# One forward pass on Trainium2: first loads reordered, 128-row matmuls in the mLSTM heads, another PEER chunk order, matmuls without a reader in two norms

## The chip, the cores and the metric

The kernel runs on one core of one Trainium2 chip, as one program. The metric is the device time of that program in microseconds. The core has five engines that work from queues of their own: TensorE (PE in the rows, with its weight loads as PEld), VectorE (DVE), ScalarE (ACT), GpSimd (POOL) and SyncE (SP, which here issues almost all loads). TensorE multiplies into PSUM; a weight load puts a stationary operand of up to 128 rows by 128 columns into the array, and a matmul streams a moving operand of up to 512 columns through it.

## What is computed

The reference runs 256 tokens of width 1024 in float32 through two blocks. The first block has two layers: a mixer (an mLSTM in layer 0, latent attention in layer 1), a layer norm over the residual, a PEER feed-forward with its own norm, and a gated per-layer embedding. The second block is a hybrid attention and a SwiGLU feed-forward. Cut to the parts that the change touches:

```python
def mlstm_mixer(x, w_in, b_if, hn_g, w_out):          # 8 heads, q and k of 64, v of 128
    proj = x @ w_in                                   # q, k, v, input and forget gate, output gate
    b = cumsum(log_sigmoid(forget gate))              # the kernel: all 256 tokens in one go
    log_w[t, s] = b[t] - b[s] + ig[s], s <= t         # M[t] = running max of ig - b
    qk = (q @ k.T) * exp(log_w - m)                   # per head, causal
    h = (qk @ v) / max(|sum(qk)|, exp(-m))
    return (sigmoid(og) * head_norm(h)) @ w_out

x = layer_norm(ALPHA * x + mix, ln_g, ln_b)           # "norm 0" after layer 0's mixer, "norm 2" after layer 1's

def peer_ffn(x, w_q, sub_keys, u, v):                 # once per layer, 16384 experts
    ...                                               # top 16 of a product of two sets of 128 keys, 8 heads
    act = gelu(x @ u[expert])
    out = sum(gate * act * v[expert])
```

The kernel computes PEER densely: the gate weights are put into a 16384 x 256 matrix that is zero where an expert wasn't picked, and all experts are run through it.

## The kernel before

Nearly all matrix products are float32 products of three passes: `split` (line 127) rounds a tile to `hi` on ScalarE and forms the rest `lo` on VectorE (or GpSimd), both of type fp32r, and `mm3` (line 153) adds hi·hi, hi·lo and lo·hi with lines 159, 160 and 161. A few small products are plain float32 matmuls, which the hardware runs as two passes each. Weights come in slabs of 1 MB: `prep` (line 131) loads a slab on SP's queue into one of three `raw` buffers and splits it in two halves, into 8 `hi` and 7 `lo` buffers. `linT` (a slab stationary, 256 tokens moving) and `linN`/`accN` (tokens stationary, 512 columns of a slab moving) consume them.

The code is straight-line Python. A framework places each instruction on its engine's queue, in an order that follows the program's order and its own estimate of readiness, and puts in the waits; buffers of a tag rotate, and a pool that is opened after another was closed may take over its memory, and then waits for its last reader. `issue_after` holds an instruction back in that ordering until another one is placed.

**The start.** `setup` (line 96) loads the small constants `vecs`. `load_x` (line 405) loads x transposed in four parts of 256 KB and splits it in eight. `trig_tables` (line 804) loads the positions and computes a table that only layer 1 needs. `mlstm` (line 414) loads the gate weights (512 KB), the q and k weights (four slabs), x again by rows (`B.X`, 1 MB) and the head norm's gain `hn` (512 KB). On TensorE it runs the gate product (24 matmuls), q and k (192), v, and then the heads. From the gate product VectorE and ScalarE make the rows `ig`, `Bc` and their running maximum `M` (lines 449 to 469).

**The heads.** `head_a` (line 493) makes for one head the exponent `lw` (line 499: `sel`, 8 rows, picks the head's row of M; line 500 adds the causal mask) and the product `qk` (line 501, 64 rows: two heads share the 128 partitions of `kT`), for two blocks of 256 and 128 columns. `head_b` multiplies by v. Between them lie three steps of the output gate's product.

**The norms.** `post_norm` (line 239) takes the two token halves (`tb`) one after the other: statistics on VectorE, normalised rows, eight transposes on TensorE (line 265), then per 128 columns the split of the transposed rows on ScalarE, VectorE and GpSimd (lines 271 to 276). With `rows` (norms 0 and 2) it also updates `B.X` on VectorE (lines 286 and 287). What follows both norms is PEER's query product `peer_w_q`, whose first slab is split before the norm and the second one after those X updates.

**PEER.** 64 chunks of 256 experts. `u_pair` makes gelu(x @ u) of a chunk (96 matmuls of 256 columns); the down product takes 24 of 512 columns. The first 25 chunks' `u_pair` (NPRE) run early, among the selection and the building of the gate matrix, and lie in `pre`. The gate matrix goes to DRAM (`wd`, 16 writes of 1 MB) and comes back in groups of four chunks (`wt`, line 783, two buffers). The last loop then takes the chunks in order: `up(j)` returns `pre[j]` or runs `u_pair`, one chunk ahead of the down product of the chunk before. In layer 0 that loop also carries 24 steps of the second block's `Ada` product, a load of 1 MB each, at every other chunk from 8 on.

Of the kernel before, what the change touches and what calls it, by code (L numbers as in the profile page):

```python
# [22 lines left out]
P = 128  # L23
# [28 lines left out]
class Builder:  # L52
# [43 lines left out]
    def setup(self):  # L96
        nc, c = self.nc, self.const
        self.ident = self.t(c, [P, P], F32, "ident")
        make_identity(nc, self.ident)
        self.vecs = self.t(c, [P, self.A["vecs"].shape[1]], F32, "vecs")  # L100
        nc.sync.dma_start(self.vecs, self.A["vecs"])
# [28 lines left out]

    def prep(self, name, s, lo_engine=None):

# [4 lines left out]
        raw = self.t(self.raw_p, [P, k, n], F32, "raw")  # L137
        self.nc.sync.dma_start(raw, src)
        if name in BY_K or k * n <= 1024 or n <= P:
# [75 lines left out]
    def rsqrt(self, var, eps, shape, tag="rs", scale=1.0):  # L215
# [13 lines left out]
        return r  # L229

    @contextmanager
    def behind(self):
# [6 lines left out]
    def post_norm(self, acc, i, rows):  # L239
# [6 lines left out]
        for tb in range(2):  # L246
# [10 lines left out]
            for h in range(2):  # L257
# [6 lines left out]
                for k in range(4 * h, 4 * h + 4):  # L264
                    nc.tensor.transpose(ps[tb, h][:, (k % 4) * P:(k % 4 + 1) * P], Y[:, tb, k * P:(k + 1) * P],
                                        self.ident)
        for tb in range(2):
# [137 lines left out]
def load_x(B):  # L405
    nc = B.nc
    B.x32 = B.t(B.state, [P, KD, S], F32, "x32")
    for k in range(0, KD, 2):
        nc.sync.dma_start(B.x32[:, k:k + 2, :], B.A["xT"][:, k:k + 2, :])
        for i in range(k, k + 2):  # L410
            B.split(B.x32[:, i, :], B.xT[0][:, i, :], B.xT[1][:, i, :])


def mlstm(B):
# [3 lines left out]
    act = B.act  # L418
    with B.pool("ml") as p, B.pool("mlw", 2) as w:
# [8 lines left out]
        sel = B.t(p, [8, 8, P], F32, "sel")  # L428
        nc.gpsimd.memset(sel, 0.0)
        nc.gpsimd.affine_select(out=sel, in_=sel, pattern=[[1, 8], [0, P]], compare_op=OP.not_equal, fill=-1.0,  # L430
                                base=0, channel_multiplier=-1)
        v.memset(va[:, :, :, 128:129], 1.0)
        hn = B.t(p, [P, D], F32, "hn")
        nc.sync.dma_start(hn, A["hn_g"].to_broadcast([P, D]))
        nc.gpsimd.tensor_scalar(hn, hn, 0.5, None, op0=OP.mult)

# [10 lines left out]
        ab = B.t(p, [32, S], F32, "ab")  # L447
        e = B.t(p, [32, S], F32, "e")
        u = B.t(p, [32, S], F32, "u")
# [8 lines left out]
        v.scalar_tensor_tensor(lf, z, 0.0, lf, op0=OP.min, op1=OP.subtract)  # L458
        zero = B.t(p, [32, S], F32, "zero")
        v.memset(zero, 0.0)  # L460
        ab2 = B.t(p, [64, S], F32, "ab2")
# [3 lines left out]
        v.tensor_tensor(ab2[0:32, :], ig, Bc, op=OP.subtract)  # L465
        M = B.t(p, [32, S], F32, "M")
# [12 lines left out]
        for tb in range(2):  # L479
# [4 lines left out]
        act(flo, tok[:, :, 32:40], AF.Exp, scale=-1.0)  # L484
        acc = B.linN(B.xT, "a_w_v")
        for tb in range(2):
# [6 lines left out]
        def head_a(h):  # L493
            r0, c = 64 * (h % 2), h // 2
# [90 lines left out]
def peer(B, li):  # L585
# [4 lines left out]
    with ExitStack() as es:  # L590
# [175 lines left out]
        with B.pool("wp", 2) as wp, B.pool("dn", 2) as dn, ExitStack() as es4:  # L766
# [7 lines left out]
            extra = Ada(B, es4.enter_context(B.pool("ada"))) if li == 0 else None  # L774
            nxt = up(0)
            last = []
            for j in range(NPAIR):
                g = nxt
                if j + 1 < NPAIR:
                    nxt = up(j + 1)  # L780
                if j % 4 == 0:
# [11 lines left out]
                last.append(((ah, al), B.slab("peer_v", li * NPAIR + j), 0, 2))  # L793
                if j != NPAIR - 2:
                    B.accN(acc, last, j == 0, j == NPAIR - 1)
                    last = []
                if extra and 8 <= j < 56 and j % 2:
                    extra.step(j // 2 - 4)
                    if j == 55:
                        extra.finish()  # L800
# [3 lines left out]
def trig_tables(B):  # L804
# [3 lines left out]
    with B.pool("tr") as p:  # L808
        pi = B.t(p, [P, S], I32, "pi")
        nc.sync.dma_start(pi, B.A["positions"].to_broadcast([P, S]))  # L810
        ang = B.t(p, [P, S], F32, "ang")
        n = B.t(p, [P, S], F32, "n")
        v.tensor_copy(ang, pi)
        v.tensor_scalar(ang, ang, B.vec("inv_freq"), None, op0=OP.mult)
        magic = 12582912.0
# [704 lines left out]
def build(tc, A, out, stages=ALL):  # L1520
    with ExitStack() as ctx:
# [3 lines left out]
        load_x(B)  # L1525
        trig_tables(B)
        if "a0" in stages:
            mlstm(B)
        else:
            B.nc.sync.dma_start(B.X, A["x"])  # L1530
        if "b0" in stages:
            peer(B, 0)
# [45 lines left out]
```

## Time and profile before

| | us |
|---|---|
| median of three runs (lowest, highest) | 2439.83 (2435.09, 2444.13) |
| the profiled execution | 2436.32 |
| its span, first to last instruction | 2434.3 |
| TensorE busy | 2354.2 (97% of the span) |
| VectorE, ScalarE, GpSimd busy | 1655.3, 1231.7, 134.2 |

In a timeline row stand the start in the span, the duration (of all that the row merges), engine, line, operation, output and inputs with their shapes, and the count; in brackets the idle time of that engine before it, and what ended that. Matmuls overlap: one of 256 columns has a duration of 0.28 us, but the next starts 0.12 us after it, so what a matmul costs is the distance between starts. A row of a table of stretches has the stretch, its length, the busy time and the count of instructions started for PE, PEld, DVE, ACT and POOL, then the granted TensorE clock as a share of 2.4 GHz, the busy share of the DMA engines and GB/s. A row of waits has who waited for whom, the sum in us, how often, and the longest.

### The profile page before, as it was taken

How to read it: one execution, taken by the hardware profiler on the slowest of the kernel's cores; microseconds unless marked ns; L12 is line 12 of the kernel's file. 1: busy time of each engine (PE TensorE's matmuls, PEld its weight loads, DVE VectorE, ACT ScalarE, POOL GpSimd, SP SyncE). 2: the span in 40 equal slices, each digit the busy share in tenths (PEclk: the TensorE clock that was granted, in tenths of full speed). 3: DMA queues.
4: the chain of work that ended last, by engine and by line, in shares of the span. 5: the costliest groups of instructions: out<-in, count | busy, mean ns of one | idle time of the engine just before them, and what ended most of it. 6: DMA issues, size and time to landing. Idle time of an engine off the chain costs nothing.

```text
span 2434.3 us, 40711 instructions
## 1 busy us (share of the span) xinstructions
PE 2354.2 (97%) x16430; PEld 2152.7 (88%) x16430; DVE 1655.3 (68%) x3164; ACT 1231.7 (51%) x1813; POOL 134.2 (6%) x117
## 2 busy tenths in 40 slices
PE   7989998999999999999999999999999999999998
PEld 6789998889999998988989888999999888789998
DVE  5679995876666665767999576555555584658554
ACT  5554555444444444745555444444444474556442
POOL 1054000000000000006300000000000010000000
PEclk9999999999999999999999999999999999999999
DMA  7333677886677664434367766655655444125543
GB/s 280 111 135 137 242 289 254 318 313 260 253 264 269 248 235 166 158 138 144 134 243 281 256 237 233 213 214 197 225 208 197 166 170 169 70 88 181 184 155 104
DMA packets 134205, 495.23 MB, mean 203 GB/s; under 512 B 8064, under 2 KB 76032, under 8 KB 80896
## 3 DMA queue, kind: packets, MB, share of 16 engines
q1 hardware_dynamic: 129120, 458.55, 52.4%
q10 hardware_dynamic: 4896, 34.08, 3.4%
q8 instruction: 128, 2.10, 0.3%
q14 instruction: 61, 0.50, 0.1%
HBM read 457.99 MB, written 34.60 MB: 202 GB/s over the span
## 4 chain that ended last, share of the span: by engine, by line
PE 47%; DVE 1%; ACT 1%; DMA 1%; issue 0%; DVEq 0%; SPq 0%; ACTq 0%
PE ps L160 9%; PE ps L161 9%; PE ps L159 9%; PE acc L159 5%; PE acc L160 5%; PE acc L161 5%; PE ps L1258 1%; PE acc L1271 0%; DMA wt<-wd 0%; PE ps L756 0%; PE acc L1144 0%; DVE lo L129 0%; PE ps L757 0%; PE ps L1259 0%; PE ps L1004 0%
## 5 line engine op out<-in xcount | busy, mean ns | idle before, releaser
L78 ACT ACTIVATE hi<-raw 128x1024 fp32r<-128x1024 f32 (+1 forms) x754 | 772.0, 1044 | 816.3 <-PE ps L160 353.7
L129 DVE TENSOR_TENSOR lo<-raw,hi 128x1024 fp32r<-128x1024 f32 (+1 forms) x714 | 865.4, 1219 | 456.6 <-PE ps L161 269.5
L159 PE MATMUL ps<-s,hi 128*128 128x256 f32 x3248 | 921.5, 285 | 15.9 <-ACT hi L78 13.3
L161 PE MATMUL ps<-s,lo 128*128 128x256 f32 x3248 | 919.4, 283 | 8.3 <-DVE lo L129 8.3
L160 PE MATMUL ps<-s,hi 128*128 128x256 f32 x3248 | 921.7, 284 | 2.0 <-DVE s L276 1.5
L159 PEld LDWEIGHTS ps<-s,hi 128*128 128x128 f32 x3248 | 615.4, 190 | 22.1 <-ACT hi L78 13.7
L161 PEld LDWEIGHTS ps<-s,lo 128*128 128x128 f32 x3248 | 615.6, 190 | 10.5 <-DVE lo L129 10.4
L160 PEld LDWEIGHTS ps<-s,hi 128*128 128x128 f32 x3248 | 616.3, 190 | 7.0 <-issue 2.0
L159 PE MATMUL acc<-hi,ah 128*128 128x512 f32 x1024 | 401.1, 392 | 10.3 <-ACT ah L78 10.2
L160 PE MATMUL acc<-lo,ah 128*128 128x512 f32 x1024 | 401.4, 392 | 0.0
L161 PE MATMUL acc<-hi,al 128*128 128x512 f32 x1024 | 400.8, 392 | 0.0
L159 PEld LDWEIGHTS acc<-hi,ah 128*128 128x128 f32 x1024 | 193.4, 189 | 49.6 <-ACT ah L78 11.5
L161 PEld LDWEIGHTS acc<-hi,al 128*128 128x128 f32 x1024 | 193.4, 189 | 41.3 <-DVE al L129 0.6
L160 PEld LDWEIGHTS acc<-lo,ah 128*128 128x128 f32 x1024 | 193.2, 189 | 37.7
L78 ACT ACTIVATE ah<-aw 128x512 fp32r<-128x512 f32 x128 | 80.3, 627 | 99.4 <-DVE aw L789 62.0
L129 DVE TENSOR_TENSOR al<-aw,ah 128x512 fp32r<-128x512 f32 x128 | 88.3, 690 | 55.4 <-ACT ah L78 54.6
L276 POOL TENSOR_TENSOR s<-x,s 128x128 fp32r<-128x128 f32 x48 | 24.3, 520 | 1545.9 <-ACT x L78 1533.2
L129 POOL TENSOR_TENSOR lo<-raw,hi 128x1024 fp32r<-128x1024 f32 x40 | 98.3, 2476 | 23.4 <-PE ps L161 12.8
L789 DVE TENSOR_TENSOR aw<-g,wt 128x256 f32<-128x256 f32 x156 | 59.3, 422 | 32.3 <-ACT g L78 32.3
L756 PE MATMUL ps<-oh,o 128*128 128x128 f16 x512 | 65.7, 220 | 9.6 <-DVE oh L750 5.3
L78 ACT ACTIVATE st<-ps 128x512 f32<-128x512 f32 x128 | 66.7, 605 | 1.8 <-ACT pre L78 1.7
L78 ACT ACTIVATE g<-ps 128x512 f32<-128x512 f32 (+1 forms) x82 | 46.5, 567 | 39.1 <-PE ps L161 39.1
(461 smaller groups left out, 2383.7 us busy)
## 6 DMA issues: line engine op xcount, KB each, us to landing
raw<-in_peer_u SPq DMA_DIRECT2D x128, 1024.0 KB, 4.8
raw<-in_peer_v SPq DMA_DIRECT2D x128, 1024.0 KB, 4.9
wd<-st ACTq DMA_DIRECT2D x32, 1024.0 KB, 4.7
wt<-wd SPq DMA_DIRECT2D x32, 1024.0 KB, 6.0
raw<-in_w_ada SPq DMA_DIRECT2D x24, 1024.0 KB, 5.2
raw<-in_peer_w_q SPq DMA_DIRECT2D x16, 1024.0 KB, 4.9
raw<-in_ffn_gate SPq DMA_DIRECT2D x11, 1024.0 KB, 4.8
raw<-in_ffn_up SPq DMA_DIRECT2D x11, 1024.0 KB, 4.8
```

Source lines behind the costliest of these rows:

```text
L78: i = self.nc.scalar.activation(out, in_, func, **kw)
L129: (lo_engine or self.nc.vector).tensor_tensor(lo, src, hi.bitcast(F32), op=OP.subtract)
L159: mm(out, lhsT[0], rhs[0], start=first, stop=False)
L160: mm(out, lhsT[0], rhs[1], start=False, stop=False)
L161: mm(out, lhsT[1], rhs[0], start=False, stop=last)
L276: lo = (v if tb and k % 2 == 0 else nc.gpsimd).tensor_tensor(xT[1][:, k, ts], x32[:, k, ts], xT[0][:, k, ts].bitcast(F32), op=OP.subtract)
L756: mm(ps[:, i * P:(i + 1) * P], o2[:, t // 2, :, t % 2], oh1[:, t // 2, :, t % 2], start=True, stop=False)
L789: v.tensor_tensor(aw[:, sl].rearrange("p (g t) -> p g t", t=16), g[:, sl].rearrange("p (g t) -> p g t", t=16), wt[:, :, (j % 4) * 2 + i, : ...
L1258: mm(o, qa[r0:r0 + 64, c, tb * P:(tb + 1) * P], kk[r0:r0 + 64, :n], start=True, stop=False)
```

## The change

- The load of `vecs` moves from `setup` into `load_x`, behind the second part of x. The gate weights are loaded first of all, on ScalarE's queue, and split before x.
- `B.X`, `hn` and `trig_tables` move behind the v product; the halving of `hn` goes from GpSimd to VectorE.
- `kT` gets one slot of 128 rows per head, of which 64 stay zero (a memset on GpSimd); q's two heads of a pair stay in `qT` as before. `sel` becomes 128 rows of fp32r, and M is split into two fp32r rows `Mp` of 128 partitions, so that line 499 runs twice, as hi and lo, and every matmul of `head_a` contracts over 128 rows.
- Tokens' transposes (`tok`) come behind the v product. Some tiles share memory (`e`, `M`, `zero`, `n`), and the pool of the heads' work tiles is closed before the one of the norm's rows is opened.
- `post_norm` 0 and 2: behind the transposes of the first token half 11 matmuls of 512 bf16 columns, behind those of the second half 4, into a PSUM buffer that nothing reads.
- Both PEER loops take the chunks in the order 28 to 31, 0 to 27, 32 to 63. `Ada`'s steps stay at the same places in the sequence.

```diff
+    def prep(self, name, s, lo_engine=None, queue=None):
...
+        (queue or self.nc.sync).dma_start(raw, src)
...
+    def stoke(self, n, after):
+        with self.tc.issue_after(after):
+            o = self.psum("acc")
+            for _ in range(n):
+                self.nc.tensor.matmul(o, self.ident_b, self.ident_b.unsqueeze(1).to_broadcast([P, 4, P]),
+                                      start=True, stop=True)
...
+                    tr = nc.tensor.transpose(ps[tb, h][:, (k % 4) * P:(k % 4 + 1) * P], Y[:, tb, k * P:(k + 1) * P],
+                                             self.ident)
+            if i % 2 == 0:
+                self.stoke(4 if tb else 11, tr.ins)
...
 def load_x(B):
+    B.prep("a_w_gate", 0, None, nc.scalar)
     for k in range(0, KD, 2):
         nc.sync.dma_start(B.x32[:, k:k + 2, :], B.A["xT"][:, k:k + 2, :])
+        if k == 2:
+            nc.sync.dma_start(B.vecs, B.A["vecs"])
...
-        for n, i in (("a_w_gate", 0), ("a_w_qk", 0)):
-            B.prep(n, i)
-        nc.sync.dma_start(B.X, A["x"])
+        B.prep("a_w_qk", 0)
-        kT = B.t(p, [P, 4, S], F32, "kT")
+        kT = B.t(p, [P, 8, S], F32, "kT")
+        nc.gpsimd.memset(kT, 0.0)
...
+        sel = B.t(p, [P, 8, P], F32R, "sel")
+        Mp = B.t(p, [P, 2, S], F32R, "Mp")
+        s32 = B.t(B.hi_p, [P, 8, P], F32, "hi")
...
+        act(sel, s32, AF.Copy)
...
+        B.split(M, Mp[0:32, 0, :], Mp[0:32, 1, :])
...
-                act(kT[:, c - 4, :], ps, AF.Copy, scale=0.125)
+                for r0 in (0, 64):
+                    act(kT[r0:r0 + 64, 2 * (c - 4) + r0 // 64, :], ps[r0:r0 + 64, :], AF.Copy, scale=0.125)
 
         B.linT(B.xT, "a_w_qk", range(4), ev_qk)
+        acc = B.linN(B.xT, "a_w_v")
+        trig_tables(B)
+        nc.sync.dma_start(B.X, A["x"])
+        hn = B.t(p, [P, D], F32, "hn")
+        nc.sync.dma_start(hn, A["hn_g"].to_broadcast([P, D]))
+        v.tensor_scalar(hn, hn, 0.5, None, op0=OP.mult)
...
-                mm(lw[:, o], sel[:, h, :], M[0:8, sb * P:], start=True, stop=False)
+                for i in range(2):
+                    mm(lw[:, o], sel[:, h, :], Mp[:, i, sb * P:], start=i == 0, stop=False)
                 mm(lw[:, sb * S:sb * S + P], B.ident_b, B.smask_b, start=False, stop=True)
-                mm(qk[:, o], kT[r0:r0 + 64, c, sb * P:(sb + 1) * P], qT[r0:r0 + 64, c, sb * P:], start=True, stop=True)
+                mm(qk[:, o], kT[:, h, sb * P:(sb + 1) * P], qT[:, c, sb * P:], start=True, stop=True)
...
+        es.close()
         with B.pool("rows") as rows:
...
+            order = [*range(28, 32), *range(28), *range(32, NPAIR)]
+            nxt = up(order[0])
             last = []
-            for j in range(NPAIR):
+            for n, j in enumerate(order):
                 g = nxt
-                if j + 1 < NPAIR:
-                    nxt = up(j + 1)
+                if n + 1 < NPAIR:
+                    nxt = up(order[n + 1])
```

## Rows read from the trace of the kernel before

**Rows 1.** What TensorE waited for, first 45 us.
```profile
PE ps L159 <- ACT hi L78: 12.0, 2, 10.1
PE ps L161 <- DVE lo L129: 3.5, 4, 1.7
```

**Rows 2.** Timeline of TensorE, start to the end of q and k.
```profile
10.11 0.58 PE L159 MATMUL ps<-s,hi 128*128 128x256 f32 x1 [10.11 <-ACT hi L78]
...
17.31 0.39 PE L161 MATMUL ps<-s,lo 128*128 128x256 f32 x1 [1.71 <-DVE lo L129]
...
43.87 0.34 PE L481 MATMUL ps<-ident,ab 64*128 64x64 f32 x2
```

**Rows 3.** Table of stretches: q and k without a wait.
```profile
31.00:43.00 12.00, 12.00 (x104) 12.00 (x104) 11.66 (x16) 9.35 (x14) 0.00 (x0) 1.00 0.75 269
```

**Rows 4.** Timelines of ScalarE and VectorE at the start.
```profile
4.57 2.26 ACT L78 ACTIVATE s<-x 128x256 fp32r<-128x256 f32 x6 [2.48 <-DMA x<-in_xT]
...
9.00 1.06 ACT L78 ACTIVATE hi<-raw 128x1024 fp32r<-128x1024 f32 x1 [0.75 <-DMA raw<-in_a_w_gate]
...
11.49 2.00 ACT L78 ACTIVATE hi<-raw 128x1024 fp32r<-128x1024 f32 x2 [1.43 <-DMA raw<-in_a_w_qk]
...
15.44 0.29 DVE L813 CAST ang<-pi 128x256 f32<-128x256 int32 x1 [4.12 <-DMA pi<-in_positions]
```

**Rows 5.** DMA rate in 40 slices of 0.3 us, first 12 us.
```profile
GB/s 0 0 0 0 0 0 155 201 171 171 212 191 205 328 376 389 348 301 280 225 239 273 212 355 451 328 492 437 451 437 437 410 382 311 297 184 89 181 44 174
```

**Rows 6.** Timeline of TensorE, one head's products (head_b, then head_a).
```profile
74.95 0.61 PE L511 MATMUL ps<-va,ex 128*128 128x129 f32 x4
75.40 0.39 PE L513 MATMUL ps<-va,ex 128*128 128x129 f32 x2
75.71 0.69 PE L499 MATMUL ps<-M,sel 8*128 8x256 f32 x2
...
76.50 0.92 PE L501 MATMUL ps<-qT,kT 64*128 64x256 f32 x4
77.35 0.48 PE L499 MATMUL ps<-M,sel 8*128 8x128 f32 x2
...
77.80 0.48 PE L159 MATMUL acc<-hi,s 128*128 128x512 f32 x1
```

**Rows 7.** Timelines of TensorE and VectorE around norm 0.
```profile
143.55 1.90 PE L265 MATMUL ps<-ident,s 128*128 128x128 f32 x8 [2.93 <-DVE s L260]
...
156.18 0.39 PE L161 MATMUL ps<-s,lo 128*128 128x256 f32 x1 [1.61 <-DVE lo L129]
...
150.10 2.62 DVE L286 TENSOR_TENSOR s<-s,gr 128x1024 f32<-128x1024 f32 x2
```

**Rows 8.** Around norm 2: timelines of TensorE and GpSimd, and a stretch.
```profile
1111.75 1.09 PE L265 MATMUL ps<-ident,s 128*128 128x128 f32 x8 [2.62 <-DVE s L260]
...
1123.70 0.39 PE L161 MATMUL ps<-s,lo 128*128 128x256 f32 x1 [0.78 <-DVE lo L129]
...
1117.79 1.37 POOL L276 TENSOR_TENSOR s<-x,s 128x128 fp32r<-128x128 f32 x1
...
1113.00:1119.00 6.00, 5.32 (x22) 4.87 (x23) 5.59 (x16) 5.74 (x14) 4.26 (x8) 0.50 0.01 3
```

**Rows 9.** Start of layer 0's PEER loop: timelines of TensorE and VectorE, a stretch.
```profile
398.14 0.80 PE L159 MATMUL acc<-hi,ah 128*128 128x512 f32 x1 [5.88 <-ACT ah L78]
...
396.66 1.43 DVE L789 TENSOR_TENSOR aw<-pre,wt 128x256 f32<-128x256 f32 x4 [3.08 <-DMA wt<-wd]
...
398.14:403.00 4.86, 4.86 (x12) 3.80 (x13) 2.69 (x6) 1.56 (x2) 0.00 (x0) 0.50 0.81 287
```

**Rows 10.** Start of layer 1's PEER loop: timeline of TensorE, a stretch.
```profile
1368.27 0.50 PE L159 MATMUL acc<-hi,ah 128*128 128x512 f32 x1 [4.34 <-ACT ah L78]
...
1369.00:1372.40 3.40, 3.40 (x9) 2.66 (x9) 1.95 (x5) 0.00 (x0) 0.00 (x0) 0.50 0.55 218
```

**Rows 11.** Table of stretches: layer 0's down products with Ada's steps.
```profile
450.00:475.00 25.00, 25.00 (x112) 20.73 (x111) 22.43 (x33) 12.43 (x15) 0.00 (x0) 1.00 0.96 339
```

More of the change, by code (lines that the diff above doesn't have):

```diff
@@ L100, in setup @@
         self.vecs = self.t(c, [P, self.A["vecs"].shape[1]], F32, "vecs")
-        nc.sync.dma_start(self.vecs, self.A["vecs"])
         self.ones = self.t(c, [P, P], F32, "ones")
@@ L129, in split @@
         (lo_engine or self.nc.vector).tensor_tensor(lo, src, hi.bitcast(F32), op=OP.subtract)
-    def prep(self, name, s, lo_engine=None):
+    def prep(self, name, s, lo_engine=None, queue=None):
         if (name, s) in self.ready:
@@ L137, in prep @@
         raw = self.t(self.raw_p, [P, k, n], F32, "raw")
-        self.nc.sync.dma_start(raw, src)
+        (queue or self.nc.sync).dma_start(raw, src)
         if name in BY_K or k * n <= 1024 or n <= P:
@@ L418, in mlstm @@
     act = B.act
-    with B.pool("ml") as p, B.pool("mlw", 2) as w:
-        for n, i in (("a_w_gate", 0), ("a_w_qk", 0)):
-            B.prep(n, i)
-        nc.sync.dma_start(B.X, A["x"])
+    with B.pool("ml") as p, ExitStack() as es:
+        w = es.enter_context(B.pool("mlw", 2))
+        B.prep("a_w_qk", 0)
         qT = B.t(p, [P, 4, S], F32, "qT")
-        kT = B.t(p, [P, 4, S], F32, "kT")
+        kT = B.t(p, [P, 8, S], F32, "kT")
+        nc.gpsimd.memset(kT, 0.0)
         va = B.t(p, [P, 2, 8, 129], F32, "va")
@@ L427, in mlstm @@
         H = B.t(p, [P, 2, 8, P], F32, "H")
-        sel = B.t(p, [8, 8, P], F32, "sel")
-        nc.gpsimd.memset(sel, 0.0)
-        nc.gpsimd.affine_select(out=sel, in_=sel, pattern=[[1, 8], [0, P]], compare_op=OP.not_equal, fill=-1.0,
+        sel = B.t(p, [P, 8, P], F32R, "sel")
+        Mp = B.t(p, [P, 2, S], F32R, "Mp")
+        s32 = B.t(B.hi_p, [P, 8, P], F32, "hi")
+        nc.gpsimd.memset(s32, 0.0)
+        v.memset(Mp.bitcast(F32), 0.0)
+        nc.gpsimd.affine_select(out=s32, in_=s32, pattern=[[1, 8], [0, P]], compare_op=OP.not_equal, fill=-1.0,
                                 base=0, channel_multiplier=-1)
+        act(sel, s32, AF.Copy)
         v.memset(va[:, :, :, 128:129], 1.0)
-        hn = B.t(p, [P, D], F32, "hn")
-        nc.sync.dma_start(hn, A["hn_g"].to_broadcast([P, D]))
-        nc.gpsimd.tensor_scalar(hn, hn, 0.5, None, op0=OP.mult)
         bif = B.vec("b_if")
@@ L447, in mlstm @@
         ab = B.t(p, [32, S], F32, "ab")
-        e = B.t(p, [32, S], F32, "e")
+        e = ab
         u = B.t(p, [32, S], F32, "u")
@@ L458, in mlstm @@
         v.scalar_tensor_tensor(lf, z, 0.0, lf, op0=OP.min, op1=OP.subtract)
-        zero = B.t(p, [32, S], F32, "zero")
-        v.memset(zero, 0.0)
+        zero1 = B.t(p, [32, 1], F32, "zero")
+        v.memset(zero1, 0.0)
+        zero = zero1.to_broadcast([32, S])
         ab2 = B.t(p, [64, S], F32, "ab2")
@@ L465, in mlstm @@
         v.tensor_tensor(ab2[0:32, :], ig, Bc, op=OP.subtract)
-        M = B.t(p, [32, S], F32, "M")
+        M = u
         v.tensor_tensor_scan(M, ab2[0:32, :], zero, 0.0, op0=OP.max, op1=OP.max)
+        B.split(M, Mp[0:32, 0, :], Mp[0:32, 1, :])
         v.tensor_tensor(Bc, Bc, M, op=OP.add)
@@ L484, in mlstm @@
         act(flo, tok[:, :, 32:40], AF.Exp, scale=-1.0)
-        acc = B.linN(B.xT, "a_w_v")
         for tb in range(2):
@@ L493, in head_a @@
         def head_a(h):
-            r0, c = 64 * (h % 2), h // 2
+            c = h // 2
             qk, lw = B.psum(), B.psum()
@@ L793, in peer @@
                 last.append(((ah, al), B.slab("peer_v", li * NPAIR + j), 0, 2))
-                if j != NPAIR - 2:
-                    B.accN(acc, last, j == 0, j == NPAIR - 1)
+                if n != NPAIR - 2:
+                    B.accN(acc, last, n == 0, n == NPAIR - 1)
                     last = []
-                if extra and 8 <= j < 56 and j % 2:
-                    extra.step(j // 2 - 4)
-                    if j == 55:
+                if extra and 8 <= n < 56 and n % 2:
+                    extra.step(n // 2 - 4)
+                    if n == 55:
                         extra.finish()
@@ L811, in trig_tables @@
         ang = B.t(p, [P, S], F32, "ang")
-        n = B.t(p, [P, S], F32, "n")
         v.tensor_copy(ang, pi)
+        n = pi.bitcast(F32)
         v.tensor_scalar(ang, ang, B.vec("inv_freq"), None, op0=OP.mult)
@@ L1525, in build @@
         load_x(B)
-        trig_tables(B)
         if "a0" in stages:
@@ L1530, in build @@
             B.nc.sync.dma_start(B.X, A["x"])
+            trig_tables(B)
         if "b0" in stages:
```

3 lines of the change are left out of this document (removed).

## The prediction, made before the changed kernel was run

> **What bounds the kernel now.** TensorE does, in 97% of the span, so I read in this order: the table of engines, what TensorE waited for, its timeline around each long wait, then the granted clock in the stretches there. A part of this change can gain in three ways only: it ends a wait of TensorE, it lets TensorE run at 2.4 instead of 1.2 GHz, or it takes TensorE less time for a product. Four places have such time. The first 45 us hold 15.5 us of waits [rows 1]. The heads run plain float32 matmuls of few rows [rows 6]. In norms 0 and 2 TensorE waits 2.9 and 2.6 us for the second token half and then runs at half clock [rows 7, 8]. Both PEER loops begin with a wait, 5.9 and 4.3 us, again with half clock behind it [rows 9, 10]. Everywhere else near these places the stretches are full [rows 11].
>
> A matmul of 256 columns costs 12.00/103 = 0.117 us at full clock [rows 3], one of 512 columns 25/112 = 0.223 [rows 11] and 3.40/8 = 0.43 at half clock [rows 10].
>
> **The start.** Before, the gate weights lie behind x on the same queue: their split starts at 9.0, the first matmul at 10.1, and the first q/k slab's `lo` is there only at 17.3, because VectorE, whose order has the trig table ahead of it, sat 4.1 us waiting for the positions [rows 2, 4]. After that q and k have two more kinds of wait: 12.0 + 3.5 us of all waits less 10.1 and 1.7 leaves 3.7 [rows 1, 2]; I leave 0.5 of it standing, as the gate's own `lo` must still be made. Stage end: 43.9 [rows 2]. Now the gate weights (0.5 MB) run beside x (1 MB). The rates add up to 1.06 MB at 6.0 us and 1.5 MB at 7.5 [rows 5]; if the two queues share alike, the gate lands near 6.0 and x near 8 (estimate from that row). ScalarE then has 1.06 for the gate and 8 x 0.38 for x [rows 4], so it is done near 10.2; the gate product of 24 matmuls, cold at about 0.21, ends between 12.0 and 13.5. The first q/k slab landed at 11.4 [rows 4]; x by rows and the positions no longer stand between the first and the second, so it lands no later. Its first half is ready 1.0 + 1.23 us behind that, at 13.6 instead of 17.3: 3.7 us. The other 3.2 us of waits go too, because the second slab is in flight from the start and is first wanted at 13.6 + 48 x 0.117 = 19.2. Together **-6.9 us**. Bounds: -3.5 if the gate's chain of ScalarE and VectorE steps puts those 3.2 us back, -8.5 if the gate product ends at 12.0 with a warm clock.
>
> What is moved lands on other queues. ScalarE's queue now holds the gate's split, which waits for its landing, ahead of x's; that is the reason for 10.2 above and not 8.3. Behind the v loads SP gets positions, x by rows and the gain, 1.65 MB or 5.5 us at 300 GB/s, ahead of the output gate's slabs, which TensorE wants only after v's 96 matmuls (21 us). VectorE's table steps come among v's splits and may wait for the positions as before, 4.1 us [rows 4]; up to 7 `lo` halves of 2.7 us of matmuls each lie ahead. Uncovered, that wait would cost its 4 us. The memset of `kT`, four more evictions, the copy of `sel` and the split of M run on engines that are half idle or idle. The norm's row loads take the heads' memory and so can't be issued before the last head; behind them on SP wait the query slabs, which are first wanted after the norm.
>
> **The heads.** One `head_a` takes 77.80 - 75.71 = 2.09 us: 0.79 for the 256-column exponent and its mask, 0.85 for `qk` (two passes over 384 columns), 0.45 for the rest [rows 6]. In the same row group a float32 product of 128 rows costs (75.40 - 74.95)/4 = 0.1125 a pass for 129 columns, that is 0.67 for `qk`'s 768, against 0.85; I read the rest as loads of few-row weights that are not hidden behind the matmul before. The exponent becomes four fp32r passes: two at 0.117, two of 128 columns, for which no row stands, between 0.059 (half of 0.117) and 0.117; I take 0.085, as the weight load need not shrink. The masks, 0.16 where the row has room for it and 0.04, I leave at 0.2. Sum 0.23 + 0.17 + 0.2 + 0.67 = 1.27, saved 0.82. One of the eight heads lies where TensorE alternates with ScalarE for the first four heads' norm, so I count seven: **-5.8 us**, bounds -3.9 to -7.6.
>
> A rule speaks against half of this. The Trainium skill, "TensorE: Matmul & The Clock Gate", section "Why this matters for your kernels", says that a single matmul of 32 contracted rows takes the same time as one of 128. By it `qk` would stay at 0.85 and a head would save 0.64, 4.5 us in all. The rows above, 0.85 for 64 rows against 0.67 worked out from 128 rows, are not the same contents, so I hold to the rows; the other way is a rival below.
>
> **The norms.** The 11 matmuls take 11 x 0.223 = 2.45 us of the waits of 2.9 and 2.6, the 4 behind the second half 0.9, before the first product that lacks an operand. So far they cost nothing. What they give: in norm 0 the clock had fallen when the second transposes ran (1.90 us for eight); in norm 2 it fell only after them (1.09) [rows 7, 8]. But TensorE's next wait is for the second slab's `lo` on VectorE, which stands behind the X updates there, 2.6 us for the first two of four [rows 7]. From the transposes to that point it is 12.63 us in norm 0 and 11.95 in norm 2, whatever TensorE's clock was in between [rows 7, 8]: the half-clock stretch behind norm 2 (6 us of it in the row) is nearly all hidden, only 0.78 us of wait was left. So warm matmuls gain at most 12.63 - 11.95 = 0.7 us in norm 0 and nothing in norm 2. Run warm, slab 0's 48 matmuls end about when GpSimd delivers the last operand, 1119.2 + 0.7 [rows 8], and TensorE waits 3.5 us until 1123.7, alike in norm 0. Waits of 2.6 to 5.9 us were each followed by half clock [rows 7 to 10]; behind one of 1.6 us the matmul took 0.39, as at full clock [rows 2, 7]. So I expect the clock to fall there, where nothing covers it: in the shorter of the two stretches at the loops, 3.4 us, TensorE ran eight matmuls at 0.43 instead of 0.223 and lost 1.6 us [rows 10]. Norm 0: -0.7 + 1.6; norm 2: +1.6; together **+2.5 us**. Bounds: -0.7 if the clock holds, +6 if both stretches last as long as the one in rows 8.
>
> **The PEER loops.** The first down product needs `wt`, which is written to DRAM and read back; it was there at 396.7, TensorE had been idle from 392.2 [rows 9]. With chunk 28 first, 2 x 96 x 0.117 = 22.5 us of `u_pair` come ahead of that product, and the wait has 17 us of room; if this cover failed, all of it would come back. The number of `u_pair` products stays. Layer 0 gains 5.88 of wait, and 11 matmuls at 0.43 instead of 0.223 (4.9 us of half clock), 2.2: 8.1 [rows 9]. Layer 1: 4.34 + 1.6 = 5.9 [rows 10]. Together **-14.0 us**, bounds -10 (some wait for the slabs of u, which now share the DMA with `wt`) to -14.5. SP gets the loads of chunks 28 and 29 ahead of `wt`; `wt` waits for the last write of `wd` in any case.
>
> **Sum.** -6.9 - 5.8 + 2.5 - 14.0 = -24.2. The profiled execution took 2436.3 (span 2434.3, 2.0 around it); that gives 2412.1. The median of the runs is 3.5 higher, and so is my forecast: **2415.5 us**.
>
> **Rivals.**
> - The clock holds in the norms, or the X updates move behind the `lo`: -0.7 to -2.5 instead of +2.5, 2411 to 2412. For it: TensorE never sits idle for all of a norm any more; against: the 3.5 us.
> - 64 or 128 rows make no difference to `qk`, and only the exponent's new passes gain: seven heads save 2.09 - (0.23 + 0.17 + 0.2 + 0.85) = 0.64 each, 1.3 us less, 2416.8. Against: 0.67 from the row group's own 128-row passes [rows 6].
> - The start and the heads give their lower bounds: +3.4 + 1.9, about 2421.
> - The loops' gain does not come: u's slabs for 28 and 29 queue with `wt` and Ada's first loads on DMA engines that are busy, and TensorE waits as before: +14, 2429.5. Against: in these loops TensorE waits for no slab [rows 11].
> - Slower than before, by the DMA: in layer 0's loop the 25 chunks that have only a down product now stand at places 4 to 28 of the order instead of 0 to 24, so ten instead of eight of Ada's loads fall among them. A chunk needs 1 MB for v, 0.25 for `wt` and 0.5 for Ada in 24 x 0.227 = 5.45 us, 337 GB/s, and DMA is busy 0.96 there [rows 11]. If the DMA gave less for long, it would be the bound: to lose the 24 us over the 21 chunks with Ada a chunk would have to take 6.6 us, below 280 GB/s, 2440 and more. Against: at 339 GB/s TensorE was full.
>
> **How the numbers follow.** Forecast 0.48, warm norms 0.20, rows without effect 0.07, lower bounds 0.11, no gain in the loops 0.10, DMA bound 0.04. All best bounds give 2436.3 - 31.3 + 3.5 = 2408.5, all worst 2428.4; runs of one kernel lie up to 4.5 apart from their median. Range 2405 to 2428. 0.5% is 12.2 us, about what a measurement of this kernel tells from no change: the first four cases lie below 2427.6, the fifth just above it, the last on the other side or short of it. Faster 0.86, same 0.11, slower 0.03.
>
> **What would show it.** First matmul before 9 us and q and k done near 37; `head_a` near 1.3 us, with `qk` at 0.67; in both norms transposes at 1.1 us, then a wait of about 3.5 us for `lo` of line 129 and a half clock behind it; no wait of line 159 for `ah` at the loops' starts and the clock full there. It is wrong if that last wait stays, if `qk` stays at 0.85, or if the down products' stretches no longer have TensorE full.

## The result, and the profile after

The changed kernel takes 2410.4 us (median of 4 runs, 2409.6 to 2413.1), the kernel before 2441.8 on the same chip: ratio 0.9878, 95% interval 0.9862 to 0.9895. Run again on another chip, it gave 0.9872 (0.9851 to 0.9893). The forecast was 2415.5, in a range of 2405 to 2428. The two profiled executions took 2436.3 and 2409.6, spans 2434.3 and 2407.8. The lines of the changed file are numbered otherwise: 158 to 160 for the three products, 128 for `lo`, 267 and 272 for the norm's last scaling and its transposes, 522 to 524 and 534, 536 for a head, 235 for the matmuls without a reader.

The change can be followed in one view: TensorE's timeline in both traces, read at the same matmul. The table says how much of the span's 26.5 us each stretch carries; 0.2 of it lie behind the last matmul. A norm counts from the transposes of its second token half to the end of the second slab, a loop from the selection's last product to its last down product.

| stretch of TensorE's program | forecast, us | the two traces, us |
|---|---|---|
| start, to v's first matmul | -6.9 | -6.8 |
| v and the heads | -5.8 | -7.0 |
| the second half of the heads' norm | 0 | +1.8 |
| norm 0 and the second query slab | +0.9 | +0.8 |
| PEER selection of layer 0 | 0 | +2.8 |
| PEER loop of layer 0 | -8.1 | -8.1 |
| from there to norm 2 | 0 | -1.1 |
| norm 2 and the second query slab | +1.6 | +1.5 |
| from there to the loop of layer 1 | 0 | -0.9 |
| PEER loop of layer 1 | -5.9 | -6.2 |
| from there to the feed-forward stage | 0 | -0.3 |
| the last feed-forward stage | 0 | -3.0 |

The start. First what TensorE waited for in 45 us (sum, times, longest), then its timeline (start, duration, in brackets the idle time before and who ended it); [rows 1, 2] are their counterparts.

```profile
PE ps L158 <- ACT hi L78: 7.4, 1, 7.4
PE ps L160 <- DVE lo L128: 1.4, 2, 0.9
```

```profile
7.35 0.58 PE L158 MATMUL ps<-s,hi 128*128 128x256 f32 x1 [7.35 <-ACT hi L78]
...
20.49 0.39 PE L160 MATMUL ps<-s,lo 128*128 128x256 f32 x1 [0.89 <-DVE lo L128]
...
37.33 0.39 PE L158 MATMUL acc<-hi,s 128*128 128x512 f32 x1
```

Waits fell from 15.5 to 8.8 us, and v starts at 37.33 instead of 44.14. The first product with the first q/k slab's `lo` starts at 13.23 instead of 17.31, 4.1 us sooner; the other 2.7 us come behind it.

One head, TensorE's timeline again, against [rows 6]:

```profile
67.19 0.39 PE L536 MATMUL ps<-va,ex 128*128 128x129 f32 x2
67.33 0.48 PE L522 MATMUL ps<-Mp,sel 128*128 128x256 f32 x2
67.66 0.23 PE L523 MATMUL ps<-smask_b,ident_b 128*128 128x128 bf16 x1
67.72 0.87 PE L524 MATMUL ps<-qT,kT 128*128 128x256 f32 x4
68.45 0.44 PE L522 MATMUL ps<-Mp,sel 128*128 128x128 f32 x2
68.73 0.23 PE L523 MATMUL ps<-smask_b,ident_b 128*128 128x128 bf16 x1
68.77 0.48 PE L158 MATMUL acc<-hi,s 128*128 128x512 f32 x1
```

By the distance of starts, `qk` takes 0.73 instead of 0.85, the gate row with its masks 0.71 instead of 1.24, and the values' last products 0.14 instead of 0.31, because what follows them no longer has few rows.

The norms, against [rows 7, 8]: transposes of the second token half and first `lo` of the second slab, in norm 0 and in norm 2, then two stretches (length; busy time of TensorE, its weight loads, VectorE, ScalarE and GpSimd; granted clock; DMA share; GB/s).

```profile
131.62 1.06 PE L272 MATMUL ps<-ident,s 128*128 128x128 f32 x8 [0.67 <-DVE s L267]
...
143.48 0.39 PE L160 MATMUL ps<-s,lo 128*128 128x256 f32 x1 [1.95 <-DVE lo L128]
...
1094.20 1.09 PE L272 MATMUL ps<-ident,s 128*128 128x128 f32 x8 [0.25 <-DVE s L267]
...
1106.16 0.39 PE L160 MATMUL ps<-s,lo 128*128 128x256 f32 x1 [2.01 <-DVE lo L128]
```

```profile
144.90:148.30 3.40, 3.40 (x19) 3.40 (x18) 3.40 (x2) 0.00 (x0) 3.40 (x2) 0.50 0.80 271
1107.50:1110.90 3.40, 3.40 (x18) 3.40 (x18) 3.40 (x2) 0.00 (x0) 3.40 (x2) 0.50 0.73 258
```

The transposes run warm, the wait for `lo` is there, 2.0 us and not 3.5, and half clock lies behind it with TensorE full. In norm 0 of this trace GpSimd's last operand of the first slab is there at 138.95 (it starts at 137.57 and takes 1.38), and the slab's last product starts at 141.01, 2.1 us behind it.

The PEER loops, against [rows 9, 10]: the first down product of each loop, and stretches of layer 0's; the last of them is down products but for some ten matmuls.

```profile
395.48 0.40 PE L158 MATMUL acc<-hi,ah 128*128 128x512 f32 x1
...
1358.58 0.40 PE L158 MATMUL acc<-hi,ah 128*128 128x512 f32 x1
```

```profile
395.00:400.00 5.00, 5.00 (x26) 4.20 (x25) 2.68 (x4) 2.18 (x3) 0.00 (x0) 1.00 0.63 236
400.00:425.00 25.00, 25.00 (x158) 22.58 (x157) 16.46 (x20) 12.69 (x15) 0.00 (x0) 1.00 0.61 208
470.00:560.00 90.00, 90.00 (x402) 74.67 (x401) 76.17 (x107) 44.31 (x52) 0.00 (x0) 1.00 0.93 334
```

No wait for `ah` is left, and TensorE is full at full clock. Adding Ada's loads to more chunks with only a down product costs nothing: [rows 11] had 112 matmuls in 25 us at 339 GB/s, the like stretch of after 402 in 90 us at 334.

### The profile page after: what moved, and what is told of

It is laid out like the page before. It is cut to its first block, busy times and chain, and to the rows that moved or that the text cites. A ratio compares the mean times of both kernels' runs of the same rounds, so it can differ in the third digit from the quotient of the medians.

```text
span 2407.8 us, 40769 instructions
## 1 busy us (share of the span) xinstructions
PE 2347.5 (97%) x16460; PEld 2149.2 (89%) x16460; DVE 1653.6 (69%) x3167; ACT 1231.8 (51%) x1818; POOL 134.1 (6%) x117
## 4 chain that ended last, share of the span: by engine, by line
PE 46%; DVE 2%; ACT 1%; issue 1%; DMA 0%; DVEq 0%; ACTq 0%
PE ps L159 9%; PE ps L160 9%; PE ps L158 9%; PE acc L158 5%; PE acc L159 5%; PE acc L160 5%; PE ps L1284 1%; DVE lo L128 0%; PE acc L1297 0%; PE acc L1170 0%; PE ps L780 0%; DMA raw<-in_peer_u 0%; PE ps L1285 0%; PE ps L1030 0%; ACT s L78 0%
## 5 line engine op out<-in xcount | busy, mean ns | idle before, releaser
L128 POOL TENSOR_TENSOR lo<-raw,hi 128x1024 fp32r<-128x1024 f32 x40 | 98.1, 2477 | 26.1 <-PE ps L160 15.9
```

Of the source, the lines that this page charges most:

```text
L128: (lo_engine or self.nc.vector).tensor_tensor(lo, src, hi.bitcast(F32), op=OP.subtract)
```

## Experiments

### The PEER order alone

The kernel before, with the loop over `order`; the places in the loop, Ada's too, are counted as in the change (cut here):

```diff
-            nxt = up(0)
+            order = [*range(28, 32), *range(28), *range(32, NPAIR)]
+            nxt = up(order[0])
...
```

> The kernel before with the new order of PEER chunks alone. My theory: both waits for ah at the loops' starts (5.88 and 4.34 us) and the half clock behind them go and nothing else changes, -14.0 us, 0.9943 of before. Rival: the slabs of u for the first chunks share the DMA with wt, or the stretch with down products alone becomes bound by the DMA: -10 or less, 0.996 or more.

Measured: 2428.5 us, ratio 0.9923 (0.9894 to 0.9953). From the last matmul of the selection to the last down product, layer 0 took 581.8 instead of 590.3 us and layer 1 587.1 instead of 593.3: -8.5 and -6.1. That settles the loops: the term is the order's, and it needs nothing else of the change. The whole gained 15.7 us in the medians, less in the profiled pair, since its clock fell in the heads, where that of before did not. Its four executions lie between 2417.7 (granted clock 0.994) and 2430.4 (0.987): two executions of one kernel can lie 12.7 us apart with the granted clock, about as much as the whole of this term.

### The start in parts

In the changed kernel the start's three moves are undone: the gate's weights back behind x on SP, the trig table and its positions early, x by rows behind the first q/k slab. The five kernels below combine them.

```diff
-    B.prep("a_w_gate", 0, None, nc.scalar)
...
-        B.prep("a_w_qk", 0)
+        for n, i in (("a_w_gate", 0), ("a_w_qk", 0)):
+            B.prep(n, i)
```

```diff
         load_x(B)
+        trig_tables(B)
...
         acc = B.linN(B.xT, "a_w_v")
-        trig_tables(B)
```

```diff
         B.prep("a_w_qk", 0)
+        nc.sync.dma_start(B.X, A["x"])
...
-        nc.sync.dma_start(B.X, A["x"])
         hn = B.t(p, [P, D], F32, "hn")
```

> The changed kernel with the gate's weights back behind x on the sync queue; the trig table stays late. My theory: the first matmul starts at 10 instead of 7.35, and since TensorE is full from there to v, the 2.7 us stay: v starts near 40. Rival: the lo of the first query slab is the later one anyway, and takes 1.4 of it back (its wait after the gate's product goes): v starts at 38.6 or before.

> The changed kernel with the trig table, and its load of the positions, back ahead of the gate's and the queries' weights; the gate's weights stay on their own queue. My theory: VectorE stands at the positions ahead of the first lo halves, the first product with lo waits 2 to 4 us longer, and what TensorE loses there it does not get back: v starts at 39 to 41 instead of 37.3, the whole 2412 to 2415 us. Rival: VectorE has room, the wait is hidden by the gate's product, and v starts within 0.5 us of 37.3.

> The changed kernel with both the gate's weights behind x and the trig table early; x by rows stays late. Alone, the first put v's start at 39.2 instead of 37.3, the second at 35.7. Theory A (the two hang together: only where the gate comes late does VectorE's wait for the positions stand ahead of the first query slab's lo): v starts at 42 to 44, nearly all of the old 44.1. Theory B (the effects add): v starts at 37.5 to 39.5, and the rest of the old start is x by rows between the query slabs.

> The changed kernel with the load of x by rows back behind the first query slab on the sync queue. Theory A: 1 MB more ahead of the second query slab delays it by 3 us or less, which the first slab's 5.6 us of matmuls hide: v starts within 0.7 us of 37.3. Theory B: TensorE waits for the second slab, v starts at 39.5 to 42.

> All three moves of the start undone (gate, trig table, x by rows), the rest of the change in place. If these three are the whole of the start's gain, v starts at 43.5 to 44.5 as in the kernel before; if the kernel's other edits at the start (the gain row's load, the products' order) carry a part, at 42 or less.

| undone | first matmul | v starts | first values of a head | v's end to first values | the whole |
|---|---|---|---|---|---|
| nothing | 7.35 | 37.33 | 66.75 | 7.1 | 2410.4, again 2408.6 |
| gate | 10.80 | 39.22 | 68.64 | 7.1 | 2408.8 |
| trig | 7.32 | 35.69 | 66.67 | 8.5 | 2407.6 |
| gate and trig | 10.58 | 40.13 | 70.97 | 8.5 | 2412.4 (one execution) |
| x by rows | 7.45 | 41.64 | 71.09 | 7.1 | 2413.6 (one execution) |
| all three | 11.14 | 44.39 | 75.23 | 8.5 | 2415.7 (one execution) |

All three together put v's start where before has it (44.39 against 44.14), so the three moves account for the start's gain. There the parts add: the gate 1.9, the trig table 0.9 more where the gate is late, x by rows 4.3, 7.1 of 7.1 us. For the gate alone, 3.45 us of a later start became 1.9, between the two expectations: TensorE waits less for `lo` afterwards. For the trig table alone both theories fell: v even starts 1.6 us earlier. VectorE's wait for the positions is 1.9 us there and stands behind both `lo` halves of the first slab; with a late gate it is 3.6 us and stands ahead of them, as in [rows 4], and TensorE waits 0.77 for the first. That is theory A's mechanism, but 40.13 lies outside of what either theory gave.

The first values show something else besides. In all three kernels with an early table it takes 8.5 instead of 7.1 us from v's end to them, since TensorE waits 0.56 and 0.28 for ScalarE at the first exponents. That takes back what the early table gave, and is 1.4 of the 2.3 us that it costs at the first values behind a late gate. Before needs 8.4 us there, with products of few rows and without these waits; that its first values come at 74.95, near the 75.23 of all three, proves nothing.

Over the whole kernel, the gate and the table alone can't be told from the changed kernel, and the 2412 to 2415 us that were expected for the table did not come.

For x by rows theory B holds; TensorE's timeline and a stretch of that kernel:

```profile
23.05 0.39 PE L160 MATMUL ps<-s,lo 128*128 128x256 f32 x1 [3.20 <-DVE lo L128]
```

```profile
24.00:27.50 3.50, 3.50 (x19) 3.50 (x18) 3.44 (x5) 2.79 (x3) 0.00 (x0) 0.51 0.44 126
```

The second slab's `lo` is late, TensorE waits 3.20 instead of 0.89 us, and 3.4 us of half clock follow: 2.3 + 1.7 of the 4.3. The half clock is not needed for the 4.3, though. With all three undone, x by rows costs as much (40.13 to 44.39) at full clock, in three waits of 1.79, 0.76 and 0.56 us, of which the first is shown, with the stretch around its end; the granted clock is 1.00 from 18.2 to 44.3. Before has the like three, 1.87, 0.75 and 0.56, also at full clock.

```profile
25.21 0.38 PE L158 MATMUL ps<-s,hi 128*128 128x256 f32 x1 [1.79 <-ACT hi L78]
```

```profile
25.00:30.00 5.00, 3.60 (x26) 3.19 (x26) 2.66 (x3) 4.93 (x8) 0.00 (x0) 1.00 0.07 26
```

### Few rows in the heads, types unchanged

```diff
-                    mm(lw[:, o], sel[:, h, :], Mp[:, i, sb * P:], start=i == 0, stop=False)
+                    mm(lw[:, o], sel[0:8, h, :], Mp[0:8, i, sb * P:], start=i == 0, stop=False)
-                mm(qk[:, o], kT[:, h, sb * P:(sb + 1) * P], qT[:, c, sb * P:], start=True, stop=True)
+                mm(qk[:, o], kT[r0:r0 + 64, c, sb * P:(sb + 1) * P], qT[r0:r0 + 64, c, sb * P:], start=True, stop=True)
```

With that, `kT` has its four slots again, without the memset and with one eviction for two heads.

> The changed kernel, with the products of the heads back on few contracted rows: 8 for the gate row (still two float32r passes over the split M) and 64 for the keys. Passes, columns and number types are those of the changed kernel, so it tells rows from types. My theory (weight loads of few rows are not hidden): qk of one head takes 0.85 instead of 0.73 us, the gate row's passes 0.1 to 0.3 longer per head, the product behind the head's values waits 0.18 for the first of them; 8 heads, 2 to 5 us in all, 2413 to 2416. Rival (rows do not matter, as the Trainium skill's rule on few rows has it): each line of a head lasts as with 128 rows, the whole within 1 us of the changed kernel. In the kernel before with the new PEER order alone, the clock fell among the heads; should it fall here too, and not with 128 rows, another 3 to 4 us.

Measured: 2415.3 us, ratio 0.9909 (0.9886 to 0.9933); on the same chip the changed kernel gave 2408.6, and the intervals overlap, so the trace must tell. The same head:

```profile
67.06 0.39 PE L534 MATMUL ps<-va,ex 128*128 128x129 f32 x2
67.37 0.50 PE L520 MATMUL ps<-Mp,sel 8*128 8x256 f32 x2
67.81 0.23 PE L521 MATMUL ps<-smask_b,ident_b 128*128 128x128 bf16 x1
67.97 0.92 PE L522 MATMUL ps<-qT,kT 64*128 64x256 f32 x4
68.81 0.43 PE L520 MATMUL ps<-Mp,sel 8*128 8x128 f32 x2
69.18 0.23 PE L521 MATMUL ps<-smask_b,ident_b 128*128 128x128 bf16 x1
```

Every line is longer: the gate row 0.44 and 0.37 instead of 0.33 and 0.28, its first mask 0.16 instead of 0.06, `qk` 0.84 instead of 0.73, and 0.31 instead of 0.14 ahead of it. Together that is 0.58 us a head, and by the starts of the last head's product 4.15 us have gathered since the first values. So rows carry about 0.6 of the 0.8 us a head, types the rest, and the rival that rows do not matter falls here. The clock did not fall in the heads.

Where the time goes can be seen in the two traces at the load of the gate row's first weights. It takes as long either way, 0.18 us with 8 rows and 0.19 with 128. But with 8 rows it begins at 67.37, 0.20 us behind the values' last product (67.17), and in the changed kernel at 67.31, together with that product (67.30). So the theory's unhidden loads are in the trace, but only at a change of the number of rows: within `qk` the third and fourth load begin with the product before them in both kernels.

### The matmuls without a reader, and what stands ahead of `lo`

Three kernels: the changed one without `stoke`; with the X updates moved behind the first `lo` half of the second slab; with both.

```diff
-            if i % 2 == 0:
-                self.stoke(4 if tb else 11, tr.ins)
```

```diff
-            self.split(raw[:, ks, ns], hi, lo, lo_engine)
+            i_lo = self.split(raw[:, ks, ns], hi, lo, lo_engine)
+            if mid and not parts:
+                mid(i_lo.ins)
...
+                def update(lo1):
+                    with self.tc.issue_after(lo1):
+                        for tb in range(2):
+                            v.tensor_tensor(X[:, tb, :], Y[:, tb, :], gr, op=OP.mult)
+                            v.tensor_tensor(X[:, tb, :], X[:, tb, :], br, op=OP.add)
...
+                self.prep("peer_w_q", 4 * i + 1, mid=update)
```

> The changed kernel without the matmuls that nobody reads, in both norms. My theory (they cost more than they give): the eight transposes of the second token half take 1.9 us in norm 0 again, the half clock that begins there lies ahead of the wait for the second slab's lo and is hidden by it, that wait shrinks from 1.95 and 2.01 us to 1 or less, and no half clock follows it; from the first transposes of a norm to the end of the second slab it is 0.8 to 1.7 us less per norm, the whole 2407 to 2409 us. Rival (the matmuls pay, by a warm clock in the norm): each norm gets longer by 0.8 us or more, the whole 2412 or more.

> The changed kernel, with the first lo half of the second query slab ahead of the X updates on VectorE, in norms 0 and 2. It tells whether the wait for lo and the half clock behind it come from that order. My theory: lo takes 1.2 us and is there at about 138.6 in norm 0 instead of 143.4, TensorE goes on without a wait and at full clock; 2.0 of wait and 1.7 of half clock go in each norm, up to 1.8 of it comes back as shorter waits for the next lo halves, which stand behind the X updates now; 2403 to 2407 us. Rival: VectorE is simply behind with its sum of work, the same wait stands one half slab later and the clock falls there: 2409 to 2412 us.

> The same order on VectorE without the matmuls that nobody reads. My theory: with the lo wait gone nothing hides the cold clock any more, so here the matmuls matter: at least one stretch of half clock lies open in each norm, 1.7 to 3.4 us each, and the whole is 3 to 7 us longer than with them. Rival: the clock in the norms is not set by these matmuls, and the time is that of the kernel with them, within 1 us.

> The version that was fastest so far once more: the changed kernel with the first lo half of the second query slab ahead of the X updates and without the matmuls that nobody reads. If its lead over the changed kernel is real, its ratio to the kernel before is 0.983 to 0.985 again, against 0.987 to 0.988 for the changed kernel; if it came from where the clock happened to fall, it is 0.986 or more.

| kernel | median, us | ratio to before, 95% |
|---|---|---|
| changed, two chips | 2410.4, 2408.6 | 0.9878, 0.9872 |
| without the matmuls | 2412.5 | 0.9871 (0.9853 to 0.9889) |
| X updates behind `lo` | 2406.6 | 0.9851 (0.9833 to 0.9869) |
| both | 2404.6 | 0.9838 (0.9821 to 0.9855) |
| both, another chip | 2406.7 | 0.9870 (0.9842 to 0.9899) |

Without the matmuls, the transposes and `lo` of both norms:

```profile
131.21 1.94 PE L272 MATMUL ps<-ident,s 128*128 128x128 f32 x8 [3.04 <-DVE s L267]
...
143.88 0.39 PE L160 MATMUL ps<-s,lo 128*128 128x256 f32 x1 [1.84 <-DVE lo L128]
...
1095.55 1.09 PE L272 MATMUL ps<-ident,s 128*128 128x128 f32 x8 [2.62 <-DVE s L267]
...
1107.51 0.38 PE L160 MATMUL ps<-s,lo 128*128 128x256 f32 x1 [0.73 <-DVE lo L128]
```

The transposes are cold again in norm 0, and from the first transposes to `lo` it takes 16.9 instead of 16.1 us; in norm 2 it is 15.9 either way, as [rows 8] let one expect. Half clock followed the wait in norm 0, and none the shorter one in norm 2. So the matmuls give 0.8 us in norm 0; in norm 2 they give nothing and only make the wait for `lo` longer, 2.0 instead of 0.7 us, with half clock behind it in both traces of the changed kernel. My theory held in norm 2 and failed in norm 0, where the wait did not shrink to 1 us and the half clock behind it stayed. The rival's 0.8 us came in norm 0 only. Over the whole kernel the 2412.5 is as the rival had it, but before is slower on that chip too (2444.2), and by the ratios nothing can be told.

With the X updates moved (line 300; 162 is the product with `lo`), the timelines of VectorE and TensorE, and two stretches:

```profile
136.65 1.25 DVE L128 TENSOR_TENSOR lo<-raw,hi 128x1024 fp32r<-128x1024 f32 x1 [0.37 <-ACT hi L78]
137.82 2.35 DVE L300 TENSOR_TENSOR s<-s,gr 128x1024 f32<-128x1024 f32 x2
...
143.63 0.39 PE L162 MATMUL ps<-s,lo 128*128 128x256 f32 x1 [0.42 <-DVE lo L128]
```

```profile
130.00:135.00 5.00, 3.84 (x23) 2.81 (x24) 3.82 (x12) 4.87 (x14) 3.19 (x7) 1.00 0.00 0
140.00:150.00 10.00, 9.57 (x81) 9.37 (x80) 9.94 (x20) 4.03 (x8) 7.50 (x4) 1.00 0.51 145
```

The wait of 2 us is gone, half a slab later one of 0.42 is left, and the clock stayed full. From the first transposes to the end of the second slab it is 3.0 us less than in the changed kernel's first trace in each norm. Half of that is the wait, and shown to come from the order on VectorE: against the traces in which no half clock followed the wait (norm 0 in the changed kernel's second trace, for one) it is 1.5 us less. The other half is a fall of the clock that did not come, and that can miss with the wait too, as the last experiment shows.

Without the matmuls the same order gives 2.2 and 2.8: they are worth 0.8 and 0.2 us, and not the 3 to 7 that I expected. The clock does fall there: in norm 0 it is 0.50 from 130.2 to 137.0 us, with TensorE busy for 5.62 of them. These 6.8 us of half clock begin as TensorE's wait of 3.0 us for the norm ends, and lie on transposes and products that wait for the norm's operands one by one: at full clock TensorE is busy for 3.84 of the 5 us from 130. The version with both was fastest in one comparison (2404.6) and ahead of the changed kernel by 2 to 6 us in the medians, but the second comparison gave 0.9870, on the side that the expectation called chance, and its interval holds both kernels; I take it as no slower, not as shown faster.

### The changed kernel once more

> The changed kernel itself once more. In its first trace the matmuls of 256 columns in the last feed-forward stage followed each other 3% faster than in the kernel before and in four of its relatives, 3.1 us in all, at the same granted clock; the change does not touch that stage. If this belongs to the kernel (where its tiles and instructions lie), it is there again; if to the execution or the chip, the stage takes as long as before here, and the whole is 2411 to 2414 us.

Measured: 2408.6 us. The last feed-forward stage in 15 us stretches, in order: before, changed, changed once more. For the last, the stretch around norm 0's wait stands first, and the wait itself below.

```profile
2288.00:2303.00 15.00, 15.00 (x126) 15.00 (x126) 7.93 (x12) 7.06 (x11) 0.00 (x0) 1.00 0.51 180
```

```profile
2263.00:2278.00 15.00, 15.00 (x130) 15.00 (x129) 8.33 (x12) 7.33 (x12) 0.00 (x0) 1.00 0.50 170
```

```profile
143.00:149.00 6.00, 5.40 (x45) 5.41 (x46) 6.00 (x4) 0.22 (x1) 6.00 (x4) 1.00 0.66 220
...
2263.00:2278.00 15.00, 15.00 (x126) 15.00 (x126) 8.41 (x13) 7.08 (x11) 0.00 (x0) 1.00 0.54 199
```

```profile
143.60 0.39 PE L160 MATMUL ps<-s,lo 128*128 128x256 f32 x1 [1.99 <-DVE lo L128]
```

126 matmuls against 130 in 15 us, at the same granted clock and with TensorE full in each: the 3 us did not come again with the same kernel, so they belong to executions and not to the change. Of all fourteen traces the quicker pace stands in two, the changed kernel's first and that of few rows in the heads (again 130, from 2266 to 2281 us at a granted clock of 1.00); I have no cause for it. And the wait of 1.99 us in norm 0 had no half clock behind it this time. The whole, 2408.6, is below the 2411 to 2414 that were expected if the pace did not come again.

## Why the prediction was right or wrong

- *The loops* were right in mechanism and size: -14.0 forecast, -8.1 and -6.2 in the two traces, -8.5 and -6.1 for the order alone. The cover of 22 us held, and so the fear of a DMA-bound stretch was idle.
- *The start* was right in its sum, and near in its parts: the first slab's `lo` came 4.1 us sooner (forecast 3.7), and 2.7 us were gained behind it (forecast 3.2). Undone one by one, up to v, the gate is worth 1.9, the table 0.9 with a late gate, x by rows 4.3. "First matmul before 9 us and q and k done near 37" came as written.
- *The heads* gained 7.0, near the bound of 7.6. Term by term the working was off: 1.44 us instead of 1.27 for `head_a`, `qk` 0.73 instead of 0.67. What made up for it had no term, and is luck: the values' products ahead of it end 0.17 sooner, and the eighth head gains as well. The choice of the rows over the Trainium skill's rule ("TensorE: Matmul & The Clock Gate", section "Why this matters for your kernels") was borne out: in this stream of products 0.84 with 64 rows, 0.73 with 128. A matmul by itself, of which the rule speaks, was not run.
- *The norms*: +2.5 forecast, +2.3 in the trace, but partly by luck. The wait was over-sized (3.5 against 2.0), at its beginning and not at its end: `lo` is used 11.9 and 12.0 us behind the transposes, as the working had it, but the first slab's last product starts 2.1 us behind GpSimd's last operand, where the working ended the slab 0.7 behind it. And the step "so I expect the clock to fall there" is too sure: in the eight traces with these matmuls and a wait of 1.9 to 2.0 us in both norms, half clock followed in norm 0 four times and in norm 2 twice. With 6 of 16 the term is near +0.5 (-0.7 and 6/16 x 2 x 1.6).
- *What had no term* comes to -0.7 in all, the sum of larger parts of either sign. At the heads' norm 1.4 of the +1.8 is 3.4 us of half clock that before lacks. In layer 0's selection 1.5 of the +2.8 is half clock and 0.9 a wait of 0.79 us for ScalarE that the one trace of before lacks and the other thirteen have, 0.6 to 2.6 us, that of the order alone among them; whether it comes with the order was not tested. The -1.1 ahead of norm 2 comes from 3.4 instead of 10.2 us of half clock, less longer waits; the -0.9 behind it are shorter waits, the -3.0 at the end is the pace. Which wait is followed by half clock changed from one execution to the next.
- *The step from the profiled execution to the median* missed most: +3.5, where the profiled run of after lies only 0.9 below its median. That is 2.6 of the 5.1 us between forecast and result. The working took a distance of before's runs for a constant; it also read their spread a little small, 4.5 for 4.7 us. In 21 further executions before had a granted clock of 0.984 to 0.990, the changed kernel in 8 of 0.991 to 0.996; the medians differ by 31, the profiled pair by 26.8. Which part of the change keeps the clock higher is open: the order alone had 0.987 to 0.994, few rows in the heads 0.990 to 0.995, the kernel without the matmuls that nobody reads 0.987 to 0.991.

## What to carry to other kernels

Where an operand must travel far (here through DRAM and back), put work that does not need it between its producer and the first reader; here the price of such a wait in the trace, with the half clock behind it, was a forecast within some tenths of a us. Loads that nobody needs soon do not belong between the first slabs of weights, and products with few contracted rows in a row of full ones were worth padding with zeros here, where the load of their weights began late. Filling TensorE's wait is worth little while another wait stands behind it: look first at what is queued ahead of the operand that it will need next.

## What the runs showed of the hardware

The fall of the clock is not a function of the kernel: the wait of 2 us in norm 0 was followed by 3.4 us of half clock in one execution of the changed kernel and by none in another, and executions of one kernel lie up to 13 us apart. Two of fourteen traces ran the 256-column matmuls of a stage 3% closer together at the same granted clock.

VectorE's subtraction of 128x1024 slows beside GpSimd's. The two groups are of the changed kernel, from 142.2 to 143.4 and from 146.8 to 149.0 us, the columns busy time and mean ns; below them is GpSimd's timeline, with two of its own.

```profile
L128 DVE TENSOR_TENSOR lo<-raw,hi 128x1024 fp32r<-128x1024 f32 x2 | 2.3, 1210 | 0.0
...
L128 DVE TENSOR_TENSOR lo<-raw,hi 128x1024 fp32r<-128x1024 f32 x2 | 6.7, 3399 | 0.0
```

```profile
143.94 6.18 POOL L128 TENSOR_TENSOR lo<-raw,hi 128x1024 fp32r<-128x1024 f32 x2
```

1.2 against 3.4 us for the same instruction. The Trainium skill, "SBUF — State Buffer", section "SBUF: two separate sides", says that a VectorE operation with two inputs in SBUF and a GpSimd operation that reads SBUF lock each other out for a whole instruction. The trace agrees: GpSimd's two run from 143.94 to 146.80 and from 146.76 to 150.13 us, VectorE's beside them from 144.49 to 147.88 and from 147.81 to 151.21, so each of VectorE's ends 1.1 us behind GpSimd's, about the 1.2 us that it takes alone.
